# Slot-wise buffers, later mixer steps and a timeline model for the order of the free engines, in a two-layer hybrid decoder step

## Chip, cores and metric

The kernel runs on one core of one Trainium2 chip. The metric is device microseconds (us) of one execution, as the median of repeated runs. One execution was taken with the hardware profiler; its trace gives every instruction's start, duration and releaser. TensorE is written PE (PEld for its weight loads), VectorE DVE, ScalarE ACT, GpSimd POOL, SyncE SP.

## The reference, cut

Two layers; in each, one input projection feeds three mixers that run over the same 1024 prompt tokens and 8 sequences of 4 new tokens. Their outputs go into one output projection and a layer norm.

```python
def mixer_layer(x, ...):                       # x: 1024 prompt + 8*4 sample tokens, d_model 1024
    proj = x @ w_in                            # 5900-odd columns, split into the inputs of all mixers
    y_ssd = rms_norm(ssd_scan(conv(xbc), dt, a, b, c, h0) * silu(z))        # 16 heads x 64, chunk 128
    q = (rms_norm(cq) @ w_uq); ckv = rms_norm(mla_ckv); kr = rope(mla_kr)
    o_lat = mla_attention(q_nope @ w_uk, rope(q_rope), [cache, ckv], [cache_rope, kr])   # cache: 8192 tokens
    y_mla = (o_lat @ w_uv) * silu(gate)
    o = gdn_scan(l2(q), l2(k), v, g, beta, s0) # 4 heads x 128, delta rule in blocks, triangular solve
    y_gdn = rms_norm(o) * silu(z)
    return layer_norm(alpha * x + concat(y_ssd, y_mla, y_gdn) @ w_out)
```

## The kernel before

All activations are held transposed, with channels on the 128 partitions and the 1056 tokens on the free axis, in three blocks of 384, 384 and 288 columns (`BLOCKS`). Products that need full precision are made of three fp32r matmuls on a high and a low part of each operand (`mm3`); `split` makes the parts, with an ACT cast for the high one and a subtraction on POOL or DVE for the low one. A tile framework assigns the waits and orders the instructions of each engine: by a list scheduler with priorities (`high_priority` lifts the instructions in its block), except on the engines that `manual_schedule` names, which keep the order in which the program emits them. The engines left to the scheduler are called free here.

**Phase 1** of a layer (`phase1`, L535) puts three generators together in `merge` (L397), which fixes PE's order by hand. Two streams, a and b, are the mixers: gated DeltaNet heads 0 and 2, the latent norms (`mla_in`) and SSD group 0 in a; the norm of the input, heads 1 and 3, the DeltaNet sample step and SSD group 1 in b. After each step a stream yields a number of us that it wants to pass before its next step, counted on a clock of emitted PE columns, or a set of things that must be done first. A third generator, `fill`, is taken whenever no stream is due: the 46 weight chunks of the input projection (PSUM banks `pj`, two of them), then the queries' up-projection (`mla_q`, L1246), the keys and values (`mla_kv`), and between them `absorb` (L1377), which makes the sample queries for decoding. PE takes its queue in order, so a step that is emitted before its input is ready holds up what stands behind it.

The steps that the change moves or lifts: the reciprocal root of a norm (`rstd`, L306), the 32-wide levels of the triangular solve in `gdn_block` (L788 to L794), the chain over four chunks there (L829, L836), its closing transpose, the opening of `ssd` (L1016 to L1029), and the first sample state in `ssd_sample`.

**Phase 2** (`phase2`, L1402) is attention. `weave_decode` (L431) emits `decode` (32 units of 2048 cached tokens; POOL gathers three units ahead into three tiles `dec_v`, DVE transposes into `dec_k`) and puts steps of the prompt's attention (`mla_prompt`) between: each number that `decode` yields is an amount of attention, on the same clock, to be emitted then. PE and DVE are in hand order there. Its pool is closed after `decode_end`; then the pool of the output projection opens in the same memory: weight halves `wo` (five slots of 1024 columns; one half takes two, high and low), 32 `mix` tiles, the residual `y`, and three PSUM banks `m`. `weave` emits the first block's projection (`out_proj`) beside what is left of attention; then blocks 1 and 2 follow, with the layer norms of the block before between them. In names of the trace, `c` is a tile that lives through the whole program (regA among them), `p_sa` and `p_sb` are the small tiles of the two streams, `stage` those of `mla_q`, `ps_x` a PSUM tile.

## Time and profile before

| what | value |
|---|---|
| median of 3 runs | 3574.2 us (3568.78 to 3581.75) |
| the profiled execution | 3572.76 us |
| its span, first to last instruction | 3571.0 us |
| mean granted clock of PE, 1.0 being 2.4 GHz | 0.939 |
| PE busy (matmul records) | 3124.5 us, 87% |
| DVE, ACT, POOL busy | 63%, 37%, 31% |
| PE idle within the span | 3571.0 - 3124.5 = 446.5 us |

What lies around the span is 1.8 us. A group of rows names an instruction by its line, engine, operation and by the tiles it writes and reads; a wait is written as the waiting instruction, an arrow and what ended the wait. The line is often that of a helper (L153 is `tt`, L156 `stt`, L159 `act`, L165 and L153 the two halves of `split`, L180 `mm`, L150 `tp`, L136 `dma`), so tiles tell more than lines. The two layers run the same program, so most rows occur twice, some 1775 us apart.

### The profile page before, as it was taken

The numbers are of one execution on the slowest core, as the hardware profiler recorded it, in microseconds if no ns is written. First come the engines' busy times: TensorE is split into PE (matmuls) and PEld (weight loads), VectorE is DVE, ScalarE is ACT, GpSimd is POOL, SyncE is SP. The second block draws the span as 40 slices with busy tenths as digits, with TensorE's granted clock in tenths as the row PEclk, the third lists the DMA queues.
The fourth block names the chain that finished last, engine by engine and source line by source line (L and its number), as shares of the span: only waits on it lengthen the run. The fifth ranks groups of instructions, "written<-read, shape, count | busy, mean of one in ns | idle before, by whom it ended". The sixth has DMA issues, their size and how long they took to land. (4 is left out here: it accounts for less than half of the span.)

```text
span 3571.0 us, 82553 instructions
## 1 busy us (share of the span) xinstructions
PE 3124.5 (87%) x33880; PEld 2666.9 (75%) x33880; DVE 2234.9 (63%) x4646; ACT 1337.2 (37%) x3099; POOL 1124.5 (31%) x1214
## 2 busy tenths in 40 slices
PE   6889999888778988979979999898987788889797
PEld 5888988888665655559878899887886566556697
DVE  7766365687545766745586653657865466666455
ACT  5433234333133344434434332343322343434344
POOL 4434344644421211101134444355453111211000
PEclk7999999999888999989989999999998799999898
DMA  3322324555776655444424232255567755553453
GB/s 137 123 90 88 106 67 161 168 169 177 249 251 201 207 178 191 171 154 157 151 83 126 83 94 90 68 171 184 173 214 254 230 191 190 183 196 128 161 180 127
DMA packets 317070, 564.70 MB, mean 158 GB/s; under 512 B 51772, under 2 KB 218748, under 8 KB 299668
## 3 DMA queue, kind: packets, MB, share of 16 engines
q1 hardware_dynamic: 293140, 408.42, 35.9%
q0 software_dynamic: 23552, 151.01, 12.0%
q8 instruction: 266, 4.36, 0.5%
q14 instruction: 112, 0.92, 0.1%
HBM read 429.00 MB, written 130.30 MB: 157 GB/s over the span
## 5 line engine op out<-in xcount | busy, mean ns | idle before, releaser
L180 PE MATMUL ps_pj<-xh,w_r 128*128 128x384 f32 (+1 forms) x4416 | 1212.7, 342 | 50.8 <-ACT p_cv L471 17.2
L180 PEld LDWEIGHTS ps_pj<-xh,w_r 128*128 128x128 f32 x4416 | 816.1, 196 | 71.0 <-ACT p_cv L471 19.1
L180 PE MATMUL ps_pj<-xl,w_r 128*128 128x384 f32 (+1 forms) x2208 | 733.9, 332 | 4.6 <-POOL xl L153 4.0
L180 PEld LDWEIGHTS ps_pj<-xl,w_r 128*128 128x128 f32 x2208 | 432.4, 196 | 13.5 <-POOL xl L153 11.1
L180 PE MATMUL ps_m<-mix,wo 128*128 128x384 f32 (+1 forms) x2304 | 395.4, 333 | 44.1 <-DVE wo L153 19.3
L180 PEld LDWEIGHTS ps_m<-mix,wo 128*128 128x128 f32 x2304 | 385.4, 196 | 50.8 <-DVE wo L153 22.4
L156 DVE SCALAR_TENSOR_TENSOR p_cv<-p_cv,c 128x384 f32<-128x384 f32 (+1 forms) x432 | 335.0, 779 | 71.9 <-ACT p_cv L159 65.9
L180 PE MATMUL ps_dS<-dec_k,c 32*32 32x256 f32 x8192 | 314.7, 385 | 31.5 <-issue 12.8
L153 POOL TENSOR_TENSOR w_r<-w_raw,w_r 128x1024 fp32r<-128x1024 f32 (+1 forms) x98 | 233.2, 2379 | 293.5 <-ACT w_r L165 251.3
L180 PEld LDWEIGHTS ps_dS<-dec_k,c 32*32 32x32 f32 x8192 | 190.1, 106 | 135.7 <-issue 85.0
L1667 DVE STREAM_TRANSPOSE dec_k<-dec_v 128x2048 f32<-128x2048 f32 x128 | 290.9, 2282 | 0.1
L1643 POOL DMA_INDIRECT dec<-cache_k_rope,c x64 | 60.9, 951 | 566.0 <-DVE dec L1736 516.9
L153 DVE TENSOR_TENSOR wo<-c,wo 128x1024 fp32r<-128x1024 f32 x96 | 119.0, 1243 | 128.2 <-PE ps_m L180 98.3
L159 ACT ACTIVATE p_cv<-p_cv 128x384 f32<-128x384 f32 x144 | 72.8, 505 | 314.8 <-DVE p_cv L156 313.8
L1470 ACT COPY c<-ps_aT 128x512 f32<-128x512 f32 (+3 forms) x192 | 89.9, 478 | 248.0 <-PE ps_aT L150 241.2
L165 ACT CAST wo<-c 128x1024 fp32r<-128x1024 f32 x96 | 100.4, 1050 | 218.3 <-DMA c<-w_out 174.9
L1643 POOL DMA_INDIRECT dec_v<-cache_kv_latent,c x128 | 120.8, 943 | 182.9 <-PE ps_dV L180 157.6
L180 PE MATMUL ps_b<-p_b 128*128 128x128 f32 (+7 forms) x1476 | 156.8, 284 | 21.1 <-ACT p_b L1024 8.4
L1513 DVE TENSOR_REDUCE c<-ps_aS 128x1 f32<-128x512 f32 (+3 forms) x192 | 105.4, 549 | 101.7 <-PE ps_aS L180 96.3
L159 ACT ACTIVATE c<-ps_aS,c 128x512 f32<-128x512 f32 (+3 forms) x192 | 110.6, 576 | 153.7 <-DVE c L1514 138.6
L318 POOL TENSOR_TENSOR c<-c,c 128x3 f32<-128x3 f32 (+2 forms) x22 | 17.1, 783 | 472.6 <-DVE c L317 472.6
L180 PEld LDWEIGHTS ps_b<-p_b 128*128 128x128 f32 (+5 forms) x1476 | 133.6, 161 | 37.7 <-ACT p_b L1024 9.9
(325 smaller groups left out, 5601.6 us busy)
## 6 DMA issues: line engine op xcount, KB each, us to landing
c<-w_out SPq DMA_DIRECT2D x96, 512.0 KB
w_raw<-w_in SPq DMA_DIRECT2D x92, 512.0 KB
pd<-p_cv SPq DMA_DIRECT2D x164, 192.0 KB
p_b<-pd SPq DMA_DIRECT2D x66, 256.0 KB
c<-pd SPq DMA_DIRECT2D x64, 256.0 KB
q<-rowd SPq DMA_DIRECT2D x48, 256.0 KB
p_b<-rowd SPq DMA_DIRECT2D x48, 256.0 KB
pd<-p_cv SPq DMA_DIRECT2D x82, 144.0 KB
```

The costliest lines, as they stand in the source:

```text
L153: eng.tensor_tensor(out=out, in0=a, in1=b, op=op)
L156: self.nc.vector.scalar_tensor_tensor(out=out, in0=a, scalar=s, in1=b, op0=op0, op1=op1)
L159: self.nc.scalar.activation(out=out, in_=in_, func=func, **kw)
L165: self.nc.scalar.copy(out=hi, in_=src)
L180: return self.nc.tensor.matmul(out, lhsT=lhsT, rhs=rhs, start=start, stop=stop)
L318: nc.gpsimd.tensor_tensor(out=r[:p, u], in0=r[:p, u], in1=self.mhalf[:p, 0:1].to_broadcast([p, u.stop - u.start]), op=ALU.pow)
L1470: nc.scalar.copy(out=t[:, :w], in_=p[:, :w])
L1513: nc.vector.reduce_max(out=m, in_=ps[:, :w], axis=AX.X)
L1643: nc.gpsimd.indirect_dma_start(out=out, out_offset=None, in_=src, in_offset=bass.IndirectOffsetOnAxis(ap=idx[:, c:c + 1], axis=0))
L1667: nc.vector.transpose(T[r].rearrange("p j s k -> p j (s k)"), V[:, :, r * 128:r * 128 + 128])
```

## The change

It does these things:

- The scheduler of the free engines uses a simulated timeline (`schedule_with_timeline_sim`) rather than the plain list order.
- Later steps: after the root of a norm 5.5 instead of 2.98, before the closing transpose of a DeltaNet block 7.5 instead of 5.2, 2.5 between the three parts of the SSD opening, 7.0 instead of 2.03 before the first sample state.
- `high_priority` around the DVE and ACT steps of the triangular solve, the chunk chain, the SSD opening, and the splits of the output weights.
- `mla_q` alternates between banks `pj` and `a`; its second rotation table is loaded behind the latents. `absorb`'s loads are issued before those of `mla_prompt`, and both wait for the end of stream a.
- One pool for decode and projection, in named slots: v0 to v2, d1 to d3. When unit 29 is done, v2 is reused for four slots of weights, then v0, v1 and d1 for the `mix` tiles of block 0, split on POOL. `decode_end` works in `dec_k`'s slot and no longer closes the decode generator: it is emitted beside attention and the first block's projection. A projection that has no residual yet yields True, and `weave` goes on with attention.
- In `weave_decode` an attention step counts at least 0.45. The two waits of 2.0 ahead of the first unit are gone.
- Weight raws use three places instead of two; the projection's PSUM banks are those of decode, then also attention's.

```diff
@@ rstd
-        yield 2.98
+        yield 5.5
@@ weave
-            while due > 0 and next(second, self) is not self:
+            while due > 0:
+                if next(second, self):
+                    break
                 due, t = due - (self.clock - t), self.clock
@@ weave_decode
-                    due -= self.clock - t
+                    due -= max(self.clock - t, 0.45)
@@ phase1, fill
                 self.hole = pk
+                yield {"a"}
+                absorb = self.absorb()
+                next(absorb)
                 self.mla = self.mla_prompt(self.tq(F32R), self.regA[:, 0:4672])
                 next(self.mla)
-                absorb = self.absorb()
-                next(absorb)
@@ gdn_block (and so for Tc/Uc, vn, Sn)
-            self.tt(nc.vector, c3(Xc), c3(p), mk1(C_L1 + 32 * lv))
+            with self.tc.high_priority():
+                self.tt(nc.vector, c3(Xc), c3(p), mk1(C_L1 + 32 * lv))
...
-        yield 5.2
+        yield 7.5
@@ ssd (its copy and its product of p2 are put under high_priority)
         for t0 in (0, 4, 8):
+            if t0:
+                yield 2.5
@@ ssd_sample
-            yield 2.03
+            yield 2.03 if b else 7.0
@@ mla_q
+        banks = itertools.cycle(("pj", "a"))
-            ps = self.psum("pj")
+            ps = self.psum(next(banks))
@@ phase2
+            self.RV = itertools.cycle([lambda k=k: place(f"v{k}", 4096, F32, "dec_v") for k in range(3)])
+            def projection():
+                rw = place("v2", 4096, F32R, "wo")
+                ws = self.out_weights(itertools.cycle([rw[:, k:k + 1024] for k in range(0, 4096, 1024)]), Ring(self.regA, 4672))
+                first = [next(ws), next(ws)]
+                yield
+                for t, n, k0, k1 in (("v0", 4096, 0, 5), ("v1", 4096, 5, 10), ("d1", 4616, 10, 16)):
+                    m = place(t, n, F32R, "mix")
+                    ...
+                    self.mix_part(None, iter(Rm[2 * k0:]), 0, range(k0, k1), mix, nc.gpsimd)
+                    if t == "v0":
+                        yield
+            def tail():
+                for _ in self.decode_end(d):
+                    for _ in itertools.islice(mla, 4):
+                        yield
+                Ry[0] = place("d2", 3072, F32, "y")
+                y.extend(self.mix_rest(Ry[0], Rt, 0))
+                yield from mla
+            out = self.out_proj(ws, 0, y)
+            self.weave(tail(), out, SHARE2)
@@ decode_units
+            if k in (29, 30):
+                next(d["projection"])
@@ out_weights
+            raw = self.tok[:, :1024] if k < 2 or k % 3 == 0 else Rr(1024)
+            with self.tc.high_priority() if k > 1 else contextlib.nullcontext():
+                w = self.split(None, raw, None, hi, lo, self.nc.vector if k > 1 else self.nc.gpsimd)
@@ kernel
-    with tile.TileContext(nc) as tc:
+    with tile.TileContext(nc, schedule_with_timeline_sim=True) as tc:
```

## Rows read from the trace of the kernel before

**Rows 1.** The page, busy time, share of the span and instructions of each engine.

```profile
PE 3124.5 (87%) x33880; PEld 2666.9 (75%) x33880; DVE 2234.9 (63%) x4646; ACT 1337.2 (37%) x3099; POOL 1124.5 (31%) x1214
```

**Rows 2.** Windows: stretch, us, busy (instructions) by engine, granted clock, DMA share, GB/s.

```profile
0.00:964.00 964.00, 854.22 (x7454) 789.76 (x7454) 630.26 (x1292) 349.49 (x830) 449.64 (x488) 0.94 0.43 136
964.00:1075.00 111.00, 77.91 (x391) 65.36 (x390) 47.95 (x109) 37.82 (x89) 26.91 (x33) 0.84 0.81 268
1075.00:1541.00 466.00, 416.02 (x7806) 272.60 (x7807) 314.11 (x706) 189.97 (x496) 82.12 (x87) 0.97 0.54 181
1541.00:1600.00 59.00, 38.94 (x216) 28.08 (x216) 23.43 (x71) 21.91 (x40) 0.00 (x0) 0.77 0.58 198
2716.00:2840.00 124.00, 88.15 (x536) 71.91 (x542) 52.82 (x111) 37.35 (x88) 27.02 (x33) 0.79 0.81 261
3303.00:3360.00 57.00, 38.28 (x213) 27.79 (x214) 22.84 (x63) 22.20 (x40) 0.00 (x0) 0.79 0.52 179
```

**Rows 3.** Waits of PE's matmuls, 0 to 964 us: total us, times, longest.

```profile
PE ps_pj L180 <- ACT p_cv L471: 9.3, 3, 3.8
PE ps_a L180 <- ACT c L1024: 9.2, 1, 9.2
...
PE ps_a L180 <- DVE p_sa L153: 7.4, 5, 4.8
...
PE ps_b L180 <- DVE p_sb L153: 5.2, 6, 2.1
...
PE ps_a L180 <- DVE p_sa L829: 4.3, 3, 3.3
PE ps_b L180 <- ACT p_b L1024: 4.2, 1, 4.2
...
PE ps_a L150 <- DVE q L153: 3.5, 2, 3.3
```

**Rows 4.** Waits of PE's matmuls, 964 to 1075 us.

```profile
PE ps_a L180 <- DVE c L153: 8.9, 1, 8.9
PE ps_pj L180 <- DVE stage L153: 4.9, 4, 1.5
...
PE ps_pj L180 <- ACT stage L1295: 1.6, 1, 1.6
```

**Rows 5.** Timeline, 1020 to 1040 us: start, duration, engine, instruction, count, idle before.

```profile
1024.23 0.94 PE L180 MATMUL ps_b<-c,p_b 128*128 128x128 f32 x6
...
1025.06 8.34 SPq L136 DMA_DIRECT2D q<-qd  x14
...
1033.45 0.51 SPq L136 DMA_DIRECT2D c<-w_ukT  x1
...
1039.34 0.42 DVE L153 TENSOR_TENSOR c<-c 96x256 f32<-96x256 f32 x1 [3.76 <-DMA c<-qd]
```

**Rows 6.** Timeline of PE, 1535 to 1600 us.

```profile
1548.67 1.97 PE L150 MATMUL ps_aT<-c,c 128*128 128x128 f32 x8 [4.53 <-ACT c L1530]
...
1578.68 11.45 PE L180 MATMUL ps_m<-mix,wo 128*128 128x384 f32 x48 [9.91 <-ACT mix L165]
1592.43 0.62 PE L180 MATMUL ps_m<-mix,wo 128*128 128x384 f32 x2 [2.31 <-ACT wo L165]
```

**Rows 7.** The output weights: timeline from 1603 us, durations by tile, PE's waits 1600 to 1808.

```profile
1603.72 36.56 PE L180 MATMUL ps_m<-mix,wo 128*128 128x384 f32 x210
...
L153 DVE TENSOR_TENSOR wo<-c,wo x96: 1211/1225/2022, 1569.0 to 3544.7; 128x1024 fp32r<-128x1024 f32 x96
L165 ACT CAST wo<-c x96: 1032/1051/1061, 1567.3 to 3543.7; 128x1024 fp32r<-128x1024 f32 x96
...
PE ps_m L180 <- DVE wo L153: 10.9, 5, 4.6
```

**Rows 8.** POOL's subtractions of 384 columns: ns least/median/most, first and last start.

```profile
L153 POOL TENSOR_TENSOR xl<-p_b,xh x32: 783/1077/1325, 32.1 to 1835.0; 128x384 fp32r<-128x384 f32 x16, 128x288 fp32r<-128x288 f32 x16
```

**Rows 9.** Windows: the last us ahead of the first decode unit.

```profile
1060.40:1075.20 14.80, 7.99 (x47) 5.69 (x46) 5.65 (x27) 7.73 (x30) 6.62 (x7) 0.80 0.82 290
```

More of the change, by code (lines that the diff above doesn't have):

```diff
@@ L581, in fill, with end @@
                         yield from absorb
-            a = Stream([{0}], misc, self.gdn_head("a", 0), self.gdn_head("a", 2), self.mla_in("a"), self.ssd("a", 0))
+            def end():
+                self.done.add("a")
+                yield from ()
+            a = Stream([{0}], misc, self.gdn_head("a", 0), self.gdn_head("a", 2), self.mla_in("a"), self.ssd("a", 0), end())
             b = Stream(norm, self.gdn_head("b", 1), self.gdn_head("b", 3), self.gdn_sample("b"), self.ssd("b", 1))
@@ L828, in gdn_block @@
             vn = Q(128)
-            nc.vector.tensor_copy(out=vn, in_=p[:, :128])
+            with self.tc.high_priority():
+                nc.vector.tensor_copy(out=vn, in_=p[:, :128])
             yield 1.42
@@ L834, in gdn_block @@
             Sn = Q(128)
-            if S is None:
-                nc.vector.tensor_copy(out=Sn, in_=p[:, :128])
-            else:
-                e = (16 + h) * 16 + cc + c
-                self.stt(Sn, S, self.elast[:, e:e + 1], p[:, :128], ALU.mult, ALU.add)
+            with self.tc.high_priority():
+                if S is None:
+                    nc.vector.tensor_copy(out=Sn, in_=p[:, :128])
+                else:
+                    e = (16 + h) * 16 + cc + c
+                    self.stt(Sn, S, self.elast[:, e:e + 1], p[:, :128], ALU.mult, ALU.add)
             S = Sn
@@ new lines, in phase2 @@
+        with self.psum_pool(f"p2ps{l}", aS=2, aT=2, aO=1, dV=1) as ps, self.pool(f"p2d{l}") as pd:
+            kts = self.hole.tile([128, 4224], F32, name="dec_k", tag="hole", bufs=1)
+            place = lambda t, n, dt, name: pd.tile([128, n], dt, name=name, tag=t, bufs=1)
+            self.RV = itertools.cycle([lambda k=k: place(f"v{k}", 4096, F32, "dec_v") for k in range(3)])
+            d1, d2, d3 = (Ring(place(f"d{k}", n, F32, f"dec{k}")) for k, n in ((1, 4616), (2, 3072), (3, 608)))
+            d = {"T": [kts[:, r * 2048:r * 2048 + 2048].rearrange("p (j s k) -> p j s k", j=16, s=4) for r in range(2)],
+                 "gs": kts[:, 4096:4224], "ps": ps, "W": Ring(kts, 0, 4096)}
+            Rt, Ry = self.cso[:, 0:384], [None, W[:, 1536:4608]]
+            def projection():
[3 more added lines that the diff above has]
+                yield
+                Rm, mix = [], [[], []]
+                for t, n, k0, k1 in (("v0", 4096, 0, 5), ("v1", 4096, 5, 10), ("d1", 4616, 10, 16)):
+                    m = place(t, n, F32R, "mix")
+                    Rm += [m[:, k * 384:k * 384 + 384] for k in range(2 * (k1 - k0))]
+                    self.mix_part(None, iter(Rm[2 * k0:]), 0, range(k0, k1), mix, nc.gpsimd)
+                    if t == "v0":
+                        yield
+                d.update(Rm=itertools.cycle(Rm), mix=mix, ws=itertools.chain(first, ws))
+            d["projection"] = projection()
+            self.weave_decode(itertools.chain(self.decode_setup(d1, d2, d3, d), self.decode_units(d)), mla)
+            next(d["projection"], None)
+            ws, Rm, y = d["ws"], d["Rm"], [d["mix"]]
+            two = lambda: ps.tile([128, 1024], F32, name="ps_m", tag="dS", bufs=1)
+            self.ms = itertools.cycle([two, lambda: self.psum("dV")])
+            def tail():
[7 more added lines that the diff above has]
+            self.weave(tail(), out, SHARE2)
+            self.pkv.close()
+            if not last:
+                self.take_x(l + 1)
+            T = Ring(W, 0, 1536)
+            Rx = Ring(self.tq(F32))
+            self.ms = itertools.cycle([two, lambda: self.psum("aS"), lambda: self.psum("dV"), lambda: self.psum("aS")])
+            par = self.par[l]
+            for nb in range(3):
+                if nb:
+                    x2 = nb == 2 and not last
+                    y = [self.mix_part(Rx, Rm, nb, range(16), [[], []], nc.vector)]
+                    y.extend(self.mix_rest(None if x2 else Ry[nb % 2], None if x2 else Rt, nb))
+                    out = self.out_proj(ws, nb, y)
+                for _ in out:
+                    pass
+                if last or nb < 2:
+                    finish(self.layer_norm("aT", T, y[1], nb, par[:, P_LNG:P_LNG + 8], par[:, P_LNB:P_LNB + 8], last,
+                                           self.total("aT", y[1], y[2]), Ry[nb % 2][:, :8 * BLOCKS[nb][1]]))
@@ L1821, in decode_end, with mix_part @@
         self.dma(self.mixd[:, 8:12, SEQ:NT], y.rearrange("p (k n) -> p k n", k=4))
-    def mix_load(self, Rs, Rm, Ry, total, nb):
+    def mix_part(self, Rs, Rm, nb, ks, mix, eng):
         c0, n, _ = BLOCKS[nb]
-        mix = [[], []]
-        for k in range(16):
+        for k in ks:
             hi, lo = next(Rm)[:, :n], next(Rm)[:, :n]
```

116 lines of the change are left out of this document (42 added, 74 removed).

## Prediction

> **What bounds the kernel now.** I read the page's busy times first: PE is busy for 3124.5 of 3571.0 us and no other engine comes near it [rows 1]. So a gain has to come out of PE's 446.5 idle us, or out of the time in which its clock is low. Then I read the windows by stage [rows 2]; the reader should compare idle time and granted clock. The long mixer stage of the first layer (0 to 964) leaves 964 - 854.2 = 110 us idle at a clock of 0.94. The change-over to attention (964 to 1075) leaves 33 us in 111 at 0.84; the second layer's leaves 36 in 124 at 0.79. Decode (1075 to 1541) leaves 50 in 466 at 0.97. The change-over to the output projection (1541 to 1600) leaves 20 in 59 at 0.77, the second layer's 19 in 57 at 0.79. So the two change-overs are thin places of a dense kernel, and the low clock comes with them. Last I read what ended PE's waits: in the mixer stage they are many and short, each named by one producer [rows 3]; in the change-overs they are few and long [rows 4 to 7]. Where I have rows of the first layer alone, I take the second as like it, because it runs the same program and its two change-overs are alike.
>
> **The change, part by part.** Prices are for one layer, then doubled.
>
> *absorb ahead of the attention loads.* PE sat 8.9 us until DVE had the sample queries [rows 4]. DVE waited for their loads, and these stood on SP's queue behind the issue of 14 loads of mla_prompt, 8.34 us long; the first of absorb's loads went out at 1033.45, right after it [rows 5]. The change swaps the two. What is left is 8.9 - 8.3 = 0.6 us. The 14 loads move back by absorb's five issues, some 3 us; their first reader runs at 1060 [rows 9], so 20 us and more cover that. Gain 8.3, twice: 16.6. It would be less if the tiles that absorb writes became free later than now; the wait for stream a says nothing new here, since that stream's end is long past.
>
> *Five banks in mla_q.* PE waited 4.9 and 1.6 us for the evacuations of its products [rows 4]. With a and pj in turn a product waits for the evacuation of one further back. I take 5 of 6.5, twice: 10 (0 to 13).
>
> *SSD opening.* The copy L1024 kept PE 9.2 and 4.2 us, once for each stream [rows 3]: a bank is wanted again before the copy has emptied it. The step of 2.5 puts PE work of the projection between, and the priority brings copy and product forward. I take 10 of 13.4, twice: 20 (0 to 27).
>
> *Solve and chunk chain.* The lifted DVE steps are those that PE waits for 7.4, 5.2 and 4.3 us [rows 3], 16.9 together. Part of each is the DVE operation itself, which priority does not shorten, so I take half: 8, twice: 16 (0 to 34). What is overtaken is convolution work on DVE, which then comes later; it feeds the mixers, not PE, unless its evacuations fall behind (the rival on the other side).
>
> *Later steps.* The closing transpose waited 3.5 us for DVE [rows 3]; 2.3 more cover most of that. I take 3, twice: 6 (0 to 7), and nothing for the root's longer step. Their cost is that a stream ends later. After its last projected chunk stream b has three roots (2.5 us more each) and the first sample state (5.0): 12.6 us. Its last matmuls of the norm now run at 1024 [rows 5], and the keys' and values' products go on to 1060 [rows 9], so 35 us cover it, 26 when absorb's stall is gone. I book nothing; without that cover it costs 12.6 a layer.
>
> *Decode start.* The two waits of 2.0 go, so attention's first steps no longer stand ahead of unit 0. These 14.8 us hold 8.0 of matmul time and 6.8 of idle [rows 9]. If unit 0 has its rows by then, the idle time falls out; if its gathers land late, PE stands with nothing between. Bounds -6.8 and +8; I book +2, twice: 4, nearer to the stall since DMA is at 290 GB/s there.
>
> *The floor of 0.45.* Counted in the code, attention has 240 steps of about 113 us of clock; with the floor they count 127, so about an eighth of them leaves decode and goes into the next stage. Decode's idle time, 50 us for 32 units [rows 2], may grow by as much as the cover shrinks: an eighth is 6. Bounds -6 (less work between) and +16; I book 3, twice: 6.
>
> *Decode to projection.* Here PE stood 4.53 us for attention's last softmax, 9.91 for the mix tiles and 2.31 for a weight [rows 6], 16.8 of the 20 us of idle time [rows 2]. The cause is that decode_end, the loads of the mix tiles and the last attention steps come one after the other. Behind that, 48 projection matmuls took 11.45 us [rows 6]; at the later pace of 36.56 / 210 = 0.174 us [rows 7] they take 8.4, so the low clock cost 3.1. That is 20 + 3.1 = 23 us at stake. After the change the mix tiles are loaded when units 30 and 31 are done, and some 25 us of attention, decode_end and the first block's matmuls are emitted in turn. What is late next is POOL: 16 subtractions of 1.08 us [rows 8] are 17 us, 11 of them after unit 31, against attention steps that are there to fill. I take 15 of 23, twice: 30 (0 to 46).
>
> A row first for the move of these splits: POOL needs 1.08 us for 384 columns [rows 8], where DVE needs 1.23 for 1024 [rows 7], but POOL had nothing else to do there [rows 2]. The Trainium skill, SBUF — State Buffer, section Who interferes with whom, speaks against it: a DVE instruction with two SBUF inputs contends with a GpSimd instruction that reads SBUF, and one of them waits for the whole of the other. No row of mine shows such a pair. By that rule DVE's small steps of decode_end could be held for up to the 17 us in each layer; by the rows alone nothing is added. I keep the rows, and the rule's case would make the term above 0 and the time 30 us longer.
>
> *Weights.* In the projection PE waited 10.9 us for DVE's subtraction of a weight, up to 4.6 at a time [rows 7], where the layer norm's steps were ahead of it; the priority turns that order round. I take 5, twice: 10 (0 to 20). Four slots instead of five mean that cast and subtraction, 1.05 + 1.23 = 2.3 us, must fit between the end of one half and the end of the next. A half is 24 matmuls, 24 x 0.174 = 4.2 us with 384 columns and by columns 3.1 with 288, so 0.8 is left at the tightest. I book 4 for both layers; with one more subtraction ahead in the queue of DVE, 1.23 - 0.8 = 0.4 is lost in each of the 96 halves, about 40 us at most.
>
> *Clock.* Where idle stretches close, the clock falls less often. In 0 to 964 the clock of 0.94 means 12% of the time at 1.2 GHz, 116 us, of which at most half is lost. I count 10 for both layers (0 to 60).
>
> *The timeline model.* It reorders ACT, POOL and SP everywhere, and DVE outside decode. No row of before prices it. The nearest is the wait for the evacuations of the input projection, 9.3 us for L471 in a layer [rows 3]: it could give back about 20, or cost what the last rival says. I take 0.
>
> Gains: 16.6 + 10 + 20 + 16 + 6 + 30 + 10 + 10 = 119. Costs: 4 + 6 + 4 = 14. PE takes its queue in order, so a wait that goes often uncovers the next producer; of the 52 us of the mixer terms and mla_q I expect some 10 back. Sum: 119 - 14 - 10 = 95 us, 3572.8 - 95 = 3478 for an execution like the profiled one. The median of before is 1.4 above it, so 3479.
>
> **The rivals.** *The waits only move.* The mixers are chains; when one producer comes sooner the next is late. Then the mixer terms, mla_q, weights and clock give a quarter: absorb 17, change-over 20, 15 from the rest, less 14: 38, so 3536. For it: the largest mixer wait is only 9.3 us [rows 3]. Against it: the named producers have one cause each.
>
> *The clock gives more.* The low clock sits where idle sits [rows 2]. If the thin places close altogether (46 for the projection, 17 for absorb, 50 for the mixers and mla_q) and half of the 60 us of slow time in each mixer stage comes back, the sum is 113 + 60 - 14 = 159: 3415. The Trainium skill, TensorE: Matmul & The Clock Gate, Part 1, says that the throttled state is the default and activity releases it, which is this mechanism; the rows agree as far as 0.97 in decode against 0.77 behind it.
>
> *It does not do what it says.* Where the model's order comes out nearly as the list's, and the new costs (14, with 40 for the four slots) eat the change-over's 47, nothing that can be measured is left: 3574. About 0.3%, 11 us, is what a measurement of this kernel can tell from no change.
>
> *Slower: the free engines' order starves the projection.* In `merge` the filler's products stand in two banks; an evacuation may be late by one block's length, 24 x 0.174 = 4.2 us, less its own 0.5, before PE stops. If the model believes in durations that the chip does not keep, and lifted mixer steps on DVE and ACT run ahead of evacuations, then each that is more than 3.7 us late stops PE. 92 chunks of three blocks are 276 evacuations; if one in four is late by 2 us beyond that, it costs 138 us against a gain of 95: 3617. It decides from about 1.4 us a late evacuation. For it: L471 already costs 9.3 us, up to 3.8 at a time [rows 3]. Against it: the copies out of pj have priority now as before.
>
> **How the numbers follow.** Forecast 3479 (own range 3445 to 3515): 0.45. Waits only move: 0.20. Clock gives more: 0.14. Nothing: 0.06. Slower: 0.15. The time is that of the likeliest. The range takes in the forecast, the waits that move, nothing, most of the clock's case and the near part of the slower one: 3405 to 3600, which leaves out about 0.08 below and 0.11 above. Faster by over 0.3%: 0.45 + 0.20 + 0.14 = 0.79; within: 0.06; slower: 0.15.
>
> **What would show it.** absorb: its loads on SP ahead of the 14 of q, PE's 8.9 us gone. SSD opening: no wait on L1024 above 2 us. Solve: p_sa and p_sb below half. Change-over: 1541 to 1600 without an idle stretch over 3 us, projection matmuls between transposes of attention, clock above 0.9. Weights: no wait of several us on DVE wo; if the four slots bind, there are waits of under 1 us in every half. The slower rival shows as ps_pj waits on ACT or DVE p_cv of 50 us and more. Wrong would be the whole if PE's idle time falls by less than 40 us, and the clock's case right if the mean clock passes 0.955.

## The result, and the profile after

The changed kernel takes 3483.8 us (median of 4, 3483.2 to 3486.4) where the kernel before took 3571.5 beside it: a ratio of 0.9755, with a 95% interval of 0.9728 to 0.9781. The prediction was 3479, between 3405 and 3600. The profiled execution has a span of 3481.4 us, 89.6 less than before.

First the page's line of busy times of the changed kernel.

```profile
PE 3091.7 (89%) x33880; PEld 2621.0 (75%) x33880; DVE 2216.9 (64%) x4610; ACT 1325.7 (38%) x3099; POOL 1176.1 (34%) x1250
```

Beside [rows 1]: PE's idle time fell from 446.5 to 3481.4 - 3091.7 = 389.7, by 56.8. The other 32.8 are busy time, for the same 33880 matmuls: the mean granted clock rose from 0.939 to 0.951.

The windows of the changed kernel, with the columns of [rows 2]: the mixer stage, the change-over to attention, decode, the change-over to the projection, and the two change-overs of the second layer.

```profile
0.00:920.00 920.00, 826.34 (x7328) 771.08 (x7328) 605.27 (x1234) 341.24 (x817) 436.47 (x468) 0.95 0.42 134
920.00:1053.00 133.00, 89.11 (x497) 71.72 (x503) 70.68 (x146) 35.38 (x72) 47.42 (x53) 0.82 0.83 279
1053.00:1512.00 459.00, 400.99 (x7533) 252.63 (x7517) 294.03 (x644) 167.58 (x455) 85.56 (x88) 0.96 0.55 186
1520.00:1570.00 50.00, 50.00 (x375) 35.61 (x373) 25.24 (x84) 32.89 (x70) 10.68 (x11) 1.00 0.37 118
2624.00:2758.00 134.00, 90.52 (x486) 73.03 (x485) 70.39 (x140) 34.46 (x72) 47.52 (x53) 0.81 0.81 271
3213.00:3270.00 57.00, 52.59 (x394) 37.44 (x387) 31.37 (x117) 36.02 (x83) 14.76 (x16) 1.00 0.43 134
```

The reader is to see three things. The mixer stage is 44 us shorter, but it also holds 7454 - 7328 = 126 matmuls fewer, which stand behind it now. The change-over to attention did not close: it is 133 us long with 44 idle, where it was 111 with 33. The change-over to the projection did close: busy throughout, at full clock, where it was at 0.77 (in the second layer 4 us of 57 are idle, also at full clock).

Waits of PE's matmuls in the changed kernel, 0 to 924 us, as in [rows 3].

```profile
PE ps_pj L180 <- DVE p_cv L156: 13.0, 6, 6.2
PE ps_pj L180 <- ACT xh L165: 12.2, 5, 4.3
PE ps_b L180 <- DVE p_b L153: 10.9, 3, 9.2
PE ps_b L150 <- POOL p_b L153: 7.0, 1, 7.0
...
PE ps_pj L180 <- ACT p_cv L468: 5.2, 2, 3.6
PE ps_a L180 <- DVE p_sa L782: 4.3, 1, 4.3
...
PE ps_pj L180 <- ACT p_cv L475: 1.9, 3, 1.4
...
PE ps_b L180 <- ACT p_b L1040: 1.6, 1, 1.6
```

The copy that opened SSD (L1024, now L1040) is down from 13.4 to 1.6. Summed over all their lines, the waits for `p_sa` fell from 17.5 to 9.6 and those for `p_sb` from 5.6 to 2.5; I had named less than half as the sign, and `p_sa` misses it. Evacuations of the input projection come to 13.0 + 5.2 + 1.9 = 20 us, somewhat more than the 17.5 of the kernel before, and far from the 50 at which I would have seen the slower rival.

Where the change-over went: SP's queue, then PE, DVE and POOL of the changed kernel around the first decode unit.

```profile
981.84 0.50 SPq L136 DMA_DIRECT2D c<-w_ukT  x1
...
1006.91 9.01 SPq L136 DMA_DIRECT2D q<-qd  x14
```

```profile
1031.90 1.04 PE L180 MATMUL ps_b<-c,p_b 128*128 128x128 f32 x6 [1.09 <-POOL p_b L318]
1050.63 1.11 PE L180 MATMUL ps_dS<-dec,c 32*32 32x256 f32 x16 [17.69 <-issue]
```

```profile
1035.52 1.79 DVE L156 SCALAR_TENSOR_TENSOR p_b<-p_b,c,ps_b 128x288 f32<-128x288 f32 x4 [4.47 <-DMA p_b<-yd]
1049.82 0.71 DVE L1759 STREAM_TRANSPOSE dec<-dec 128x512 f32<-128x512 f32 x1 [12.51 <-DMA dec<-cache_k_rope,c]
```

```profile
1036.06 1.81 SPq L136 DMA_DIRECT2D mixd<-p_b  x4
```

```profile
1040.48 1.21 POOL L1680 DMA_INDIRECT dec_v<-cache_kv_latent,c  x1 [8.11 <-issue]
```

absorb's loads now go out 25 us ahead of the 14 of q, and the stall of 8.9 us at its products [rows 4] is gone. But a stall of 17.7 stands ahead of the first decode unit. Read backwards: unit 0 needs its gathered rows; POOL issues the first gather at 1040.5, 2.6 us after SP has issued the stores of stream b's last elementwise step (1035.5 to 1037.3, itself behind a reload from DRAM). The profile names no releaser for the gather, but in all 14 kernels and both layers it goes out 2.2 to 3.0 us behind the last of these stores, so I take them for what frees its memory. Stream b is late because its steps were set later (with the old steps these stores go out 4 us sooner). PE has nothing between, since attention no longer stands ahead of unit 0.

For the experiments I split a layer at three events of the trace: the start of the input projection, the first product of decode unit 0 with `dec_k`, and the last of unit 31. The sums of both layers, in us of the profiled executions:

| kernel | up to unit 0 | decode | behind it | span |
|---|---|---|---|---|
| before | 2106.6 | 910.6 | 553.8 | 3571.0 |
| changed | 2045.5 | 913.2 | 522.7 | 3481.4 |
| list_order | 2114.4 | 887.4 | 526.9 | 3528.7 |
| before_model | 2085.7 | 908.2 | 535.1 | 3529.0 |
| old_steps | 2052.5 | 923.3 | 524.3 | 3500.1 |
| old_phase2 | 2050.3 | 914.1 | 537.2 | 3501.6 |
| | | | | |
| after_again (changed) | 2042.8 | 821.6 | 524.0 | 3388.4 |
| no_lift | 2043.2 | 823.4 | 526.7 | 3393.3 |
| absorb_late | 2045.5 | 821.5 | 524.8 | 3391.8 |
| steps_absorb | 2045.4 | 818.6 | 521.6 | 3385.6 |
| steps_absorb_banks | 2056.8 | 817.5 | 524.6 | 3398.9 |
| attn_first | 2049.8 | 816.2 | 510.2 | 3376.2 |
| attn_more | 2074.8 | 820.7 | 501.6 | 3397.1 |
| act_hand | 2045.4 | 881.0 | 525.2 | 3451.6 |

The lower half ran under other conditions: the kernel before took 3506 us there, not 3578, and decode is 92 us shorter with the same program (the last section). So kernels are compared within a half, by their ratio to the kernel before of the same group. The changed kernel stands at 0.9755 in the upper half and at 0.9693 [0.9678, 0.9708] in the lower: the change is worth 88 us in the one and 0.0307 x 3506 = 108 in the other. The table shows one execution of each kernel; that of old_steps is the slowest of five (3501.9, the median being 3492.8).

The first stretch can be split once more, at the end of the input projection's last product, into mixer stage and change-over. Both layers together, in us:

| kernel | mixer stages | of it PE idle | change-overs |
|---|---|---|---|
| before | 1875.3 | 198.7 | 231.3 |
| before_model | 1878.7 | 205.5 | 207.0 |
| list_order | 1839.0 | 190.8 | 275.4 |
| old_steps | 1889.8 | 202.7 | 162.8 |
| old_phase2 | 1782.9 | 155.6 | 267.4 |
| changed | 1779.1 | 155.2 | 266.5 |
| steps_absorb_banks | 1880.3 | 202.1 | 176.5 |

### The profile page after: what moved, and what is told of

It reads as the page before. It is cut to its first block, busy times and chain, and to the rows that moved or that the text cites. A ratio compares the mean times of both kernels' runs of the same rounds, so it can differ in the third digit from the quotient of the medians.

```text
span 3481.4 us, 82579 instructions
## 1 busy us (share of the span) xinstructions
PE 3091.7 (89%) x33880; PEld 2621.0 (75%) x33880; DVE 2216.9 (64%) x4610; ACT 1325.7 (38%) x3099; POOL 1176.1 (34%) x1250
## 5 line engine op out<-in xcount | busy, mean ns | idle before, releaser
L156 DVE SCALAR_TENSOR_TENSOR p_cv<-p_cv,c 128x384 f32<-128x384 f32 (+1 forms) x432 | 359.5, 834 | 63.7 <-ACT p_cv L159 57.2
L180 PE MATMUL ps_dS<-dec_k,c 32*32 32x256 f32 x8192 | 332.1, 383 | 18.4 <-DVE dec_k L1704 2.1
L153 POOL TENSOR_TENSOR w_r<-w_raw,w_r 128x1024 fp32r<-128x1024 f32 (+1 forms) x98 | 235.1, 2400 | 242.8 <-ACT w_r L165 220.4
L180 PE MATMUL ps_dV<-dec_v,dec 128*32 128x256 f32 x2048 | 129.5, 395 | 37.5 <-ACT dec L1740 34.8
L180 PE MATMUL ps_aS<-mix,wo 128*128 128x384 f32 (+1 forms) x960 | 159.6, 322 | 1.4 <-DVE wo L153 1.4
L1717 DVE TENSOR_REDUCE dec<-ps_dS 128x1 f32<-128x512 f32 x64 | 44.2, 691 | 179.6 <-PE ps_dS L180 179.5
L153 DVE TENSOR_TENSOR wo<-c,wo 128x1024 fp32r<-128x1024 f32 x92 | 115.4, 1254 | 67.0 <-ACT wo L165 66.6
L1515 ACT COPY c<-ps_aT 128x512 f32<-128x512 f32 (+3 forms) x192 | 89.9, 478 | 177.6 <-PE ps_aT L150 157.2
L180 PEld LDWEIGHTS ps_aS<-mix,wo 128*128 128x128 f32 x960 | 152.1, 188 | 3.6 <-DVE wo L153 2.3
```

Source lines behind the costliest of these rows:

```text
L153: eng.tensor_tensor(out=out, in0=a, in1=b, op=op)
L156: self.nc.vector.scalar_tensor_tensor(out=out, in0=a, scalar=s, in1=b, op0=op0, op1=op1)
L180: return self.nc.tensor.matmul(out, lhsT=lhsT, rhs=rhs, start=start, stop=stop)
L1515: nc.scalar.copy(out=t[:, :w], in_=p[:, :w])
L1717: nc.vector.tensor_reduce(out=al, in_=s3, axis=AX.XY, op=ALU.max)
```

## The experiments

**The timeline model taken out of the changed kernel, and put alone into the kernel before.**

```diff
-    with tile.TileContext(nc, schedule_with_timeline_sim=True) as tc:
+    with tile.TileContext(nc) as tc:
```

> The changed kernel with one edit undone: the free engines are ordered by the plain list scheduler again. Theory of my sum: the timeline model is worth 0 and the parts do the work, so 3484 within 10 us (3474 to 3494). Rival one: the model carries a good part of the gain, since the mixer stages became 41 and 49 us shorter where my mixer terms came to about 25 a layer before their discount; then about 20 to 50 us come back, 3504 to 3534, with longer waits of PE for ACT and DVE p_cv. Rival two: the model costs time by its wrong durations, so that without it the kernel is 10 us or more faster, under 3474.

> The kernel before with nothing but the timeline model switched on. Theory of my sum: 0, so 3571 within 10 us. Rival: the model alone gives 20 to 50 us, 3521 to 3551. If the model helps here and its absence costs nothing in the changed kernel (or the other way round), it works only together with another part, and the difference of the two numbers says how much.

Measured: without it 0.986 [0.9841, 0.9878], so 0.0105 x 3574 = 37 us come back; alone 0.9887 [0.9866, 0.9909], a gain of 0.0113 x 3578 = 40 us. The sizes of both rivals that gave the model 20 to 50 held; the longer waits for evacuations that the first of them named did not show (21.9 us on `p_cv` without the model, 20.1 with it). The totals add up (the other edits without the model gain 1 - 0.986, some 50 us), the places do not. Without the model the other edits gain nothing ahead of unit 0 (2114.4 against 2106.6), 23 in decode and 27 behind it. The model alone gains 21 ahead of unit 0, 2 and 19. Together it is 61 ahead of unit 0, and decode loses what the list order had given it there.

What the model does in the mixer stage can be read from PE's waits in the kernel before with nothing but the model, 0 to 975 us. First all that name the streams' small tiles, then two of those that grew.

```profile
PE ps_a L180 <- DVE p_sa L153: 5.8, 1, 5.8
PE ps_a L180 <- DVE p_sa L773: 4.3, 1, 4.3
PE ps_a L180 <- DVE p_sa L829: 2.3, 2, 2.1
PE ps_a L180 <- DVE p_sa L836: 1.8, 1, 1.8
PE ps_a L180 <- DVE p_sa L156: 1.0, 2, 0.5
PE ps_b L180 <- DVE p_sb L153: 0.7, 2, 0.5
PE ps_b L180 <- DVE p_sb L836: 0.4, 1, 0.4
```

```profile
PE ps_b L180 <- DVE p_b L153: 14.1, 4, 9.3
...
PE ps_a L180 <- DVE c L153: 9.1, 1, 9.1
```

The copy L1024 (9.2 and 4.2 in [rows 3]) is gone with no step moved and no priority, and `p_sb` is down from 5.6 to 1.1. With steps and priority but without the model (list_order) the copy is down too, to 1.9. So this wait was not the lack of a gap in PE's order alone: either remedy, a better order of the free engines or a later step, removes it. But `p_sa` comes to 15.2, against 17.5 before, the wait for `p_b` L153 grew from 7.8, and that of 9.1 is new. PE's idle time in the mixer stages did not fall: 205.5 against 198.7 us. Inside this stage the waits only moved. What the model alone gains ahead of unit 0 it gains in the change-overs, 207.0 against 231.3. There absorb's stall, 8.9 us in one layer [rows 4] and 9.5 in the other, is gone, though absorb's loads are emitted where they were.

**The later steps put back.**

```diff
-        yield 5.5            # rstd
+        yield 2.98
-        yield 7.5            # gdn_block, closing transpose
+        yield 5.2
-            if t0:           # ssd
-                yield 2.5
-            yield 2.03 if b else 7.0
+            yield 2.03
```

> The changed kernel with the four later steps put back (2.98 after the root, 5.2 before the closing transpose, no 2.5 in the SSD opening, 2.03 before the first sample state). Theory of my sum: their gain is 3 a layer and their share of the SSD opening some 5 a layer, nothing is lost at the end, so 3484 + 16 = 3500. Rival one, from the trace after: the later steps lengthen stream b's tail by up to 12.6 us a layer and nothing covers that any more (PE stands 17.7 us ahead of the first decode unit), so undoing them gains up to 25 us less what the mixers lose, 3459 to 3480, and the stall ahead of the first unit shrinks below 10 us. Rival two: the shorter mixer stages (41 and 49 us) come mostly from the steps; then 30 us or more come back, over 3514.

Measured: 0.9756 [0.9741, 0.9772] against 0.9755, nothing, give or take 11 us. The theory's 16 and the second rival's 30 are out, and of the first rival's 4 to 25 only the small end is left; but it had the mechanism. Up to the last product of the first layer's input projection it takes 970 us, against 921 in the changed kernel; from there to unit 0 it takes 81, against 132. The 49 us by which the mixer stage got shorter are mixer work that the later steps move behind the projection's end, and the waits in it: with the old steps PE's idle time in the mixer stages is back at 202.7 us. The change-over as I had forecast it is to be seen here and not in the changed kernel: 970 to 1051 us.

```profile
970.00:1051.00 81.00, 69.75 (x360) 60.23 (x360) 44.60 (x85) 29.10 (x57) 21.73 (x29) 0.87 0.89 298
```

11 idle us are left of 33 [rows 2].

**Attention, decode and projection as before** (`weave`, `weave_decode`, `phase2`, the decode functions, `out_weights` and `out_proj` in the form before; too long for a diff).

> The changed kernel with attention, decode and output projection as before (own pool for the projection, two waits of 2.0 ahead of the first unit, mix tiles split on DVE behind the end of decode, five weight slots, no floor); the mixers, absorb ahead of mla_prompt's loads, and the timeline model stay. Theory of my sum: projection 30 and weights 10 are lost, 14 of costs come back, so 3484 + 26 = 3510. Rival one, from the trace after: attention to the next layer's start is 38.7 us shorter in each layer, so undoing it costs about 77: 3561, if the change-over ahead of decode stays as slow as after. Rival two: the slow change-over (133 us against 111 before) is the new phase 2's own doing, so it gets shorter by 15 to 20 a layer: 3484 + 77 - 35 = 3526.

Measured: 0.9797 [0.9779, 0.9814], 0.0042 x 3574 = 15 us back; my sum's 26 is at the end of what the intervals allow (15, give or take 11), and the two rivals are out. By stretches: 14.5 behind decode, 5 ahead of unit 0, nothing in decode. The 38.7 us of the rivals' expectation counted from attention's first step; much of it only changed sides. With attention first, attention starts at 1034.6 and unit 0 at 1055.8; in the changed kernel unit 0 comes at 1052.8 and attention behind it.

**No priority on solve, chain and SSD opening** (`high_priority` taken from the five places in `gdn_block` and `ssd`).

> The changed kernel without the priority around the steps of the solve, the chunk chain and the SSD opening; the timeline model and all else stay. Theory of my sum: 16 for solve and chain and up to 10 of the SSD opening are lost, 3484 + 16 to 26, a ratio of 0.980 to 0.983. Rival: under the timeline model these steps are placed by their modelled start and the lift changes little, ratio 0.9755 +- 0.002; the waits on p_sa L782 and p_sa, p_sb L153 stay as in the changed kernel (4.3 and under 2 in the first layer).

Measured: 0.9684 [0.9665, 0.9703], against 0.9693 with it. The rival held: nothing, give or take 8 us. The waits are those of the changed kernel to the tenth, 4.3 for `p_sa` L782 and 2.4 for L841.

**absorb behind mla_prompt's loads again; then the later steps undone as well; then mla_q's banks and its second table too.**

```diff
+                self.mla = self.mla_prompt(self.tq(F32R), self.regA[:, 0:4672])
+                next(self.mla)
                 absorb = self.absorb()
                 next(absorb)
-                self.mla = self.mla_prompt(self.tq(F32R), self.regA[:, 0:4672])
-                next(self.mla)
@@ the third kernel, besides the later steps
-        banks = itertools.cycle(("pj", "a"))
+        banks = itertools.cycle(("pj",))
```

> The changed kernel with the order of absorb and of mla_prompt's first loads swapped back (absorb's loads behind the 14 of q). Theory of my sum: 8.3 us a layer come back, a ratio of 0.980. Rival, from the trace after: the change-over no longer waits for absorb's products but for stream b's late tail and the gathers behind it (PE stands 17.7 us ahead of unit 0), so a stall of 8 at absorb shortens that one by as much and nothing is lost: 0.9755 +- 0.002.

> The changed kernel with both the later steps and the order of absorb put back. Each alone changed nothing that can be measured by stages (first decode unit at 1051, 1052 and 1053 us). Theory: they stand in for each other, since the later steps move mixer work into the place where absorb's products were waited for; then both undone cost the 8.3 a layer that my sum gave to absorb: 16 us over the control, and the first decode unit comes 8 later, at about 1060. Rival: absorb's order is worth nothing under the timeline model in any case: within 5 us of the control.

> As steps_absorb, with mla_q's products back on two banks and its second table back ahead of the latents. What is left of the change is the timeline model, the lift and phase 2. Theory of my sum: banks 5 a layer, so 10 us over steps_absorb. The ledger: the model alone gave 40 of the 88 us, undoing phase 2 cost 15, and nothing else showed a cost alone; if the other 33 are these three parts standing in for one another, this kernel is 25 to 35 us over the control, and its first decode unit comes at about 1070, near the 1074 of the model alone. Rival: they are worth little here too, and the 33 lie in an interplay of the model with phase 2: under 15 over the control.

> The changed kernel, unedited, as the control for the other three of this call and, by stages, for the four runs before. In those four the kernel before took 3506 us, not 3572, and decode (first product of unit 0 to the last of unit 31) took 411 us where the changed kernel showed 459 with the same program. If that is the supply of instructions to PE, which differs between executions of different calls (waits of PE's weight loads that nothing in the profile ends: 53 us in the first layer's decode then, 8 us in the later four), the stage up to the first decode unit is as long as ever (1052 to 1054 us), and a ratio to before between 0.967 and 0.976 comes out. If absorb's order and the lift are worth nothing, this control is within 0.2% of their ratio of 0.968 when it runs under the same supply.

Measured, the changed kernel at 0.9693: absorb late 0.9679 [0.9659, 0.9700]; with the later steps undone too 0.9658 [0.9644, 0.9671]; with one kind of bank as well 0.9715 [0.9701, 0.9728]. The control came out as expected, within 0.2% of 0.968. But the swap itself isn't tested by these runs, because it does not reach SP's queue. SP is one of the engines that the scheduler orders, and under the model absorb late has the same order of loads there as the changed kernel, absorb's first:

```profile
981.01 0.51 SPq L136 DMA_DIRECT2D c<-w_ukT  x1
...
1006.50 9.00 SPq L136 DMA_DIRECT2D q<-qd  x14
```

Both rows come within 1 us of the changed kernel's. steps_absorb and old_steps, too, issue the loads of absorb and of q in one and the same order. What is shown is that under the model it makes no difference where absorb's loads are emitted; the theory that the swap and the later steps stand in for each other fell with it. With the later steps undone as well the kernel is, if anything, faster: by 12 us, give or take 7, by the ratios, by 2.8 in the profiled spans. So the later steps may even cost a little. The banks are worth 0.0057 x 3506 = 20 us by the medians and 13 by the spans, 11 of these ahead of unit 0, where I had placed them. The ledger's theory, that the three parts hold 25 to 35 us between them, fell too: all three undone cost 8 us by the ratios, 10 by the spans. The rival's bound, under 15, held.

**Attention ahead of the first unit again.**

```diff
         d["ready"] = [d["load"](0, 0)]
+        yield 2.0
...
-        d["ready"] += [d["load"](0, 1), d["load"](0, 2)]
-        yield 0.0
+        d["ready"] += [d["load"](0, 1)]
+        yield 2.0
+        d["ready"] += [d["load"](0, 2)]
+        yield 3.5            # in attn_more alone
```

> The changed kernel with the two waits of 2.0 back ahead of the first decode unit, so that attention steps stand before it again. Theory of my sum: taking them out cost 2 a layer, so this one is 4 faster, a ratio of 0.9745 where the changed kernel has 0.9755. Rival, from the trace after: PE stands 17.7 us ahead of unit 0 because the gathers start only when stream b's tail has freed their memory; 8 us of attention would fill that place, and come out of decode's later stretch or of what follows it, so 8 to 15 a layer are gained: 0.967 to 0.971. Second rival: attention's first steps wait for the same queue, since their loads stand on SP beside absorb's; then 0.

> The changed kernel with attention ahead of the first decode unit again, 2.0 as before and 3.5 more behind the third load. With 2.0 and 2.0 PE still stood 6.5 us for the first unit's transposes and 4.2 ahead of attention. Theory: the place in front of the gathers holds as much attention as one puts there, so 12 to 20 us are gained on the control over both layers (the 17.7 us of idle time ahead of unit 0 falls under 3 us, the 4.2 ahead of attention stays). Rival: attention taken from decode uncovers decode's own waits, and the gain stays at or under 8 us.

Measured: 0.9631 [0.9612, 0.9651] with 2.0 and 2.0, so 0.0062 x 3506 = 22 us faster than the changed kernel and 3377 us in all: the version that beats both. With 3.5 more it is 0.9713 [0.9699, 0.9727], 7 slower than the changed kernel. By the profiled spans the first gains 12 us on the changed kernel and 17 on no_lift. The rival's mechanism held, and by the ratios its 16 to 30: in the first layer unit 0 comes no later (1053.0, against 1049.6 to 1053.5 in the kernels of that half that have no attention ahead of it), in the second some 4 us later than in the changed kernel, and the attention put ahead of it is missing behind decode, 510.2 against 524.0. My theory for the second, that the place holds any amount, fell. DVE's rows there, in hand order:

```profile
1064.04 0.29 DVE L156 SCALAR_TENSOR_TENSOR c<-ps_aO,c 128x128 f32<-128x128 f32 x1 [15.93 <-DMA c<-gated]
...
1064.40 0.71 DVE L1762 STREAM_TRANSPOSE dec<-dec 128x512 f32<-128x512 f32 x1
```

The added attention got as far as a step on DVE that waits for a load of `gated`, which SP issues after the gathers have begun; unit 0's transposes stand behind that step, and unit 0 comes at 1067.4.

**ACT in hand order during decode.**

```diff
-        with self.tc.manual_schedule(engines={mybir.EngineType.PE, mybir.EngineType.DVE}):
+        with self.tc.manual_schedule(engines={mybir.EngineType.PE, mybir.EngineType.DVE, mybir.EngineType.Activation}):
```

> The changed kernel with ACT kept in the emitted order during decode, as PE and DVE are already (one more engine named in the manual schedule around the decode loop). From the traces of the first four runs: decode takes 459 us from the first product of unit 0 to the last of unit 31 in the changed kernel, 444 under the list scheduler, and PE's wait for the copy L1740 of the turned weights is 18.7 us against 3.3; in the changed kernel that copy stands on ACT behind an attention activation whose reciprocal comes late from DVE. Theory, the model's order of ACT is what costs decode its 15 us: both layers gain 12 to 15, a ratio to the kernel before of 0.9675 +- 0.002 where the changed kernel has 0.9755, and the wait on L1740 falls under 5. Rival, the emitted order only moves the wait to attention's own activations (the waits on L1515 and L1575 grow by as much) or the first units' late start makes the difference: ratio 0.974 to 0.977.

Measured: 0.9853 [0.9833, 0.9873], 0.016 x 3506 = 56 us slower. The theory fell, and the rival's bound was too small as well. The wait on L1740 did shrink, from 19.1 to 5.7 in the first layer's decode; the copies of attention's weights out of PSUM, L1515, took its place.

```profile
PE ps_aO L180 <- ACT c L1515: 26.9, 19, 2.5
PE ps_aT L180 <- ACT c L1515: 17.1, 11, 3.1
PE ps_aT L150 <- ACT c L1515: 8.2, 5, 4.2
```

In the emitted order ACT holds those copies behind decode's exponential, which waits for PE; one of many places:

```profile
1195.31 0.69 ACT L159 ACTIVATE dec<-ps_dS,dec 128x512 f32<-128x512 f32 x1 [5.97 <-PE ps_aS L180]
...
1196.18 0.57 ACT L1515 COPY c<-ps_aT 128x512 f32<-128x512 f32 x1
```

So the emitted order isn't the better one. Why the list order's decode is 26 us shorter than the model's (887.4 against 913.2) stays open; the wait on L1740 is 3.3 there in the first layer, against 18.7.

## Why the prediction came out, by its own steps

The time came out to within 5 us, and the ways in which it could be seen to be wrong did not occur: idle time fell by 56.8, above the 40 named, and the clock stayed at 0.951, under the 0.955 of the clock's rival. The stretches come out too. Ahead of unit 0 I had booked 16.6 + 10 + 20 + 16 + 6 for absorb, banks and mixers, and 10 for waits that move, less 4 for decode's start: 55 with no clock, 65 with all of it; measured 61. Behind decode I had 30 + 10 - 4 = 36; measured 31. The change inside decode, 6 of cost, is measured as 2.6.

But the split is off already between the two kinds of time: of the 95, at most 16 were clock (10, and 3.1 in each change-over to the projection) and some 79 idle time; measured are 56.8 of idle time and 32.8 of busy time. And the causes to which the sum gave its sizes are mostly not the ones that the runs show.

- **The timeline model** was booked at 0 and is worth about 40 us, nearly half of the change. This is the step that failed. The nearest row that I took for it, L471 with about 20 for both layers, was one row; the model orders SP and POOL as well, and waits that come from such an order I had already given to other edits. Alone it gains 24 us in the change-overs to attention, absorb's stalls among them, and 19 behind decode, and nothing in the mixer stages, where that row lies.
- **SSD opening, solve and chain, later steps** (20 + 16 + 6): the named waits fell, but the priority is worth 0 and the later steps 0 once the model is there. With the model, the priority and all else but the later steps, PE is idle in the mixer stages for 202.7 us, where it was for 198.7: the waits only moved, as the first rival had it. The later steps do take 47 us of idle time out of these stages, but the change-overs give it back: 266.5 us against 162.8. The error was to cost each edit as if it alone could remove its wait, and as if a wait removed were time gained.
- **absorb** (16.6): the stall of 8.9 went, but by the model's order of SP's queue, not by the swap; its 16.6 are part of the model's 40. What the swap is worth without the model, no run shows; under the list order it does put the loads first, and a wait of 5.1 is left.
- **What ends the change-over** I did not ask. In the kernel before it is PE's own work: the third gather of unit 0 goes out when the products of the keys and values end (1060.6 us), and the first steps of attention follow ahead of unit 0.

```profile
1043.21 0.94 POOL L1643 DMA_INDIRECT dec_v<-cache_kv_latent,c  x1 [0.30 <-issue]
1060.89 0.95 POOL L1643 DMA_INDIRECT dec<-cache_k_rope,c  x1 [16.74 <-PE ps_aS L180]
```

So it is in the second layer, and with the model alone (products to 1056.5, third gather at 1056.8). In all the other kernels the third gather follows the second after 0.3 us. The new phase 2 is probably one way there: in the three kernels that have it with the old steps the products still run to between 1045.8 and 1048.9, but the third gather goes out at 1034.3 to 1039.3, and unit 0 comes within 2.3 us of their end. (These kernels also hold the priority and the wait for the end of stream a; no run separates the three.) The later steps are another: with the old phase 2 the products end at 1027.8, ahead of every gather. With both, as in the changed kernel, they end at 1030.3, and unit 0 waits for stream b's stores and the gathers behind them.
- **The later steps' tail at no cost**, covered by 26 to 35 us of products: wrong as it stood. Stream b's last sample states come 12 us later than with the old steps (1022.0 against 1009.6), its norm comes behind the cover, and the first gather 4 us later (1040.5 against 1036.5); the time is paid out of the mixer stage, which gets as much shorter.
- **Decode start** (+4): the sign was right. The runs put the cost at 12 (spans) to 22 us (ratios) for both layers, 6 to 11 each, where I booked 2 and allowed 8; the stall is 17.7 a layer.
- **mla_q's banks** (10): 13 to 20 with the old steps, their place as predicted.
- **Decode to projection, weights, slots, floor** (30 + 10 - 4 - 6, and -4 for the start, together 26): 15 in one piece. The change-over filled as described. PE's first products of `mix` and `wo` come between attention's steps, and waits on `wo` are under 1 us each:

```profile
PE ps_m L180 <- ACT dec L159: 2.9, 1, 2.9
PE ps_pj L180 <- ACT w_r L165: 2.8, 1, 2.8
PE ps_dV L180 <- DVE wo L153: 1.4, 2, 0.8
PE ps_aS L180 <- DVE wo L153: 1.1, 2, 0.9
```

These are PE's largest waits from 1512 to 1766 us, beside 10.9 on `wo` alone in [rows 7]; the four slots cost nothing that can be seen. What the term missed is an overlap again: of the 31 gained behind decode, the other edits give 27 without the model, and the model gives 19 without them.

The parts do not add up to shares, because they overlap. The model alone gives 40 us; the model with all but phase 2 gives 0.0203 x 3578 = 73, the whole change 88. In the other half of the table the model with the priority and phase 2, but without steps, swap and banks, gives 0.0285 x 3506 = 100 of 108. So on top of the model either group brings most of what is left, and the third gather's wait above is one that goes with either of them. The sizes are known to some 7 to 11 us each and mix the two halves, and no run puts phase 2 alone under the list order. That the sum was right is therefore largely an accident: its total came out, but not its split into idle and busy time, and most of the gains belong to other edits than those it gave them to.

The rule of the Trainium skill that I weighed, SBUF — State Buffer, section Who interferes with whom, can be seen here for the first time in this case. A DVE step of the last unit's softmax with two SBUF inputs, which takes 0.15 us elsewhere, meets POOL's splits of the mix tiles:

```profile
1512.43 4.83 POOL L153 TENSOR_TENSOR mix<-mix 128x384 fp32r<-128x384 f32 x5 [10.33 <-ACT mix L165]
```

```profile
1513.40 1.00 DVE L153 TENSOR_TENSOR dec<-dec,dec 64x1 f32<-64x1 f32 x1
```

It takes 1.00, about the length of one POOL instruction (4.83 / 5 = 0.97). The trace agrees with the rule. But it is not the only step that is held, and not only steps with two inputs are: three copies (L1807) in the same stretch take 1.78, where three of the same size behind it take 0.52.

```profile
1515.67 1.78 DVE L1807 COPY dec_k<-dec_k 32x8 f32<-32x8 f32 x3
...
1518.23 0.52 DVE L1812 COPY dec_k<-dec_k 32x8 f32<-32x8 f32 x3
```

Three more steps, attention's, are held beside POOL's next splits. The two `TENSOR_TENSOR` of 128 rows below take 0.66 and 0.92 us, where others of their line take 0.15.

```profile
1533.89 1.61 DVE L153 TENSOR_TENSOR c<-c 128x2 f32<-128x2 f32 x2 [3.13 <-ACT c L159]
...
1535.73 0.73 DVE L1571 TENSOR_SCALAR c<-c 128x2 f32<-128x2 f32 x1
```

Each held step ends 0.01 to 0.03 us after the end of a POOL instruction. Together that is about 4 us of DVE's time in the first layer, not the 17 at the rule's end, and PE has no idle time from 1520 to 1570.

## What to carry to other kernels

A wait has more than one remedy. Before the prices of several edits are added, ask of each whether another edit in the same change would remove the same wait; what is left for each is what the others don't take. A wait that is gone is time gained only if the stage got shorter and the next one not longer: compare PE's idle time of the stages, not single waits. When a stall is to be removed, follow the stage to its last releaser (in the changed kernel a gather that waits for memory) rather than to the nearest queue, and put work that is ready in front of it, up to the first step that waits for the same transfers. And see in the trace that an edit arrived: the order in which a program emits its work binds only the engines that are in hand order.

## What the runs showed of the hardware that I had not expected

The changed kernel, with the same instructions, took 3399 us in one group of runs and 3484 in another, and the kernel before 3506 and 3571 to 3578. All of the changed kernel's difference lies in decode: 821.6 against 913.2 us, where the other two stretches agree to 3. The rows of PE's weight loads in the first layer's decode say which waits differ, first the execution of 3481 us, then that of 3388.

```profile
PEld ps_dS L180 <- issue: 59.2, 123, 0.8
```

```profile
PEld ps_dS L180 <- issue: 8.6, 28, 0.4
```

In the longer execution the loads of 32x32 stop in the middle of a run, for about half a us each, with nothing in the profile that ends the wait. A single product takes the same 374 ns (median) in both. It is not the chip: one and the same chip ran four kernels of each half. Nor is it the difference between list order and model, whose stops in the first layer's decode are 61.3 and 59.2 us. The decode of the kernel before has fewer of them in the longer executions (49.2, and 45.8 in old_phase2), so the change loses there a part of what its decode gains, which may be why it is worth 20 us more in the other group; no trace of the kernel before from that group shows it. The Trainium skill, Runtime: NRT & Kernel Launch, section Instruction fetch mechanics, says that each engine fetches its instructions by a DMA queue of its own, a page at a time, and that the cost of this is mostly hidden; the instruction queue moved the same 59 packets in that stretch in both, so the trace shows no difference there, and the cause stays open.
